# Seven block products for eight in the feed-forward stage of a two-layer hybrid backbone

## The chip, the core and the metric

The kernel runs as one program on one NeuronCore of a Trainium2 chip. The metric is the device time of one execution in microseconds (us). The engines are TensorE (PE in the profile; its weight loads are PEld), VectorE (DVE), ScalarE (ACT), GpSimd (POOL) and SyncE (SP), which here issues nearly all DMAs. Tiles live in SBUF with 128 partitions; TensorE writes to PSUM, which has eight banks of 128x512 float32.

## The reference

Two layers work on 1024 latent tokens and 256 context tokens of width 1024. Each layer modulates and norms its input, projects it, runs four mixers (convolution, gated linear attention, softmax attention, retention), projects back with w_out, and adds the feed-forward stage that the change is about:

```python
def sq_relu_mlp(h, w_up, w_down):
    return jnp.square(jax.nn.relu(h @ w_up)) @ w_down
...
        x = x + g1_l * o_l
        h2_l = rms_norm(x, norm2_g[l]) * (1.0 + sc2_l) + sh2_l
        x = x + g2_l * sq_relu_mlp(h2_l, w_up[l], w_down[l])
```

w_up is 1024x4096 and w_down 4096x1024. Layer 0 does the same for the context tokens; layer 1 does not need them. After layer 1 a final RMSNorm gives the output.

## The kernel before

Everything is held transposed: 128 features on the partitions, tokens along the row. Tokens come in three groups (TOK, line 29): the context (t = 0, 256 tokens) and two latent halves (t = 1 and 2, 512 each). Products are made at float32-like precision from rounded halves: split (line 180) lets ScalarE round a tile to its high part (line 181) and VectorE subtract that from the tile to give the low part (line 182); mm3 then takes three matmuls per 128x128 weight block: high with high, high with low, low with high (all of them show as line 188).

The feed-forward stage walks the hidden axis in 16 chunks of 256 rows (FC). For each chunk and each token group, up makes two 128-row blocks of hidden values in PSUM (8 x 3 matmuls each), lets ScalarE take relu and square (lines 1146 and 1147) and VectorE a second exact square and the low part (lines 1148 and 1149); down multiplies them with all eight 128-column blocks of w_down (2 x 3 matmuls each) and VectorE adds the gated result to x in SBUF (line 1162). The hidden values never leave the core. up of the next unit is issued ahead of down of the current one, so TensorE always has a unit to work on; five PSUM banks named bank rotate. Weights come in slabs of 128x1024 (load_slab), three staging buffers and five pairs of high and low parts.

The order on each engine is set by the program's text and by a scheduler that moves an instruction forward where its operands are ready; each engine then runs its list in order, waiting for semaphores. Buffers of a pool rotate: a new tile waits until the readers of the tile that had its place are done. SyncE issues DMAs in its list's order too.

In layer 0 the modulation matrix of layer 1 is computed in between (emit_mods, step(mg, 2)), and when a token group's last chunk is done, next_norm writes its normed input for layer 1 (lines 383, 386, 387). In layer 1 final_norm transposes and stores the output (line 1190). The output projection before the stage (line 1119) works in two halves of 512 columns.

## Time and profile before

| | |
|---|---|
| median of 3 runs | 3239.86 us (3232.47 to 3243.09) |
| the profiled execution | 3238.09 us, span 3236.3 us |
| mean granted TensorE clock | 0.957 of full speed |
| TensorE busy (matmuls) | 3034.6 us, 94% of the span |
| VectorE, ScalarE, GpSimd busy | 1670.9, 913.2 and 66.4 us |
| HBM traffic | 76 GB/s over the span |

The span runs from the first to the last instruction. A row of the profile names a line, an engine, an operation, and the tiles as output<-inputs. Busy shares of TensorE are of modelled matmul lengths that overlap in the pipe, so the rate is read from start to start. The granted clock is 1.00 at 2.4 GHz and 0.50 at 1.2 GHz.

### The profile page before, as it was taken

How to read it: one execution, taken by the hardware profiler on the slowest of the kernel's cores; microseconds unless marked ns; L12 is line 12 of the kernel's file. 1: busy time of each engine (PE TensorE's matmuls, PEld its weight loads, DVE VectorE, ACT ScalarE, POOL GpSimd, SP SyncE). 2: the span in 40 equal slices, each digit the busy share in tenths (PEclk: the TensorE clock that was granted, in tenths of full speed). 3: DMA queues.
4: the chain of work that ended last, by engine and by line, in shares of the span. 5: the costliest groups of instructions: out<-in, count | busy, mean ns of one | idle time of the engine just before them, and what ended most of it. 6: DMA issues, size and time to landing. Idle time of an engine off the chain costs nothing. (4 is left out here: it accounts for less than half of the span.)

```text
span 3236.3 us, 43494 instructions
## 1 busy us (share of the span) xinstructions
PE 3034.6 (94%) x18101; PEld 2452.4 (76%) x18101; DVE 1670.9 (52%) x2660; ACT 913.2 (28%) x1650; POOL 66.4 (2%) x114
## 2 busy tenths in 40 slices
...
GB/s 265 113 74 85 128 44 79 82 203 105 33 92 85 90 84 82 85 66 36 38 32 14 99 48 36 77 50 63 167 113 79 66 45 39 48 53 52 53 39 52
DMA packets 267230, 250.31 MB, mean 77 GB/s; under 512 B 28259, under 2 KB 227513, under 8 KB 267033
## 3 DMA queue, kind: packets, MB, share of 16 engines
...
q0 software_dynamic: 416, 0.92, 0.1%
q14 instruction: 56, 0.45, 0.0%
...
## 5 line engine op out<-in xcount | busy, mean ns | idle before, releaser
L188 PE MATMUL bank<-ahi,whi 128*128 128x512 f32 (+1 forms) x2096 | 787.5, 376 | 14.6 <-ACT ahi L181 11.2
L188 PE MATMUL bank<-ahi,wlo 128*128 128x512 f32 (+1 forms) x2096 | 777.8, 372 | 2.3 <-DVE wlo L182 2.3
L188 PE MATMUL bank<-alo,whi 128*128 128x512 f32 (+1 forms) x2096 | 779.5, 372 | 0.0
L1162 DVE SCALAR_TENSOR_TENSOR x<-bank,mods,x 128x512 f32<-128x512 f32 (+1 forms) x640 | 438.8, 695 | 248.0 <-PE bank L188 247.1
L188 PEld LDWEIGHTS bank<-ahi,whi 128*128 128x128 f32 x2096 | 397.5, 190 | 103.6 <-ACT ahi L181 14.3
L188 PE MATMUL bank<-hl,whi 128*128 128x512 f32 (+1 forms) x1280 | 471.8, 369 | 0.0
L188 PE MATMUL bank<-hh,whi 128*128 128x512 f32 (+1 forms) x1280 | 471.3, 368 | 0.0
L188 PE MATMUL bank<-hh,wlo 128*128 128x512 f32 (+1 forms) x1280 | 471.0, 368 | 0.0
L188 PEld LDWEIGHTS bank<-ahi,wlo 128*128 128x128 f32 x2096 | 396.9, 190 | 73.3 <-issue 5.9
L188 PEld LDWEIGHTS bank<-alo,whi 128*128 128x128 f32 x2096 | 397.7, 190 | 67.6 <-issue 5.4
L181 ACT CAST whi<-wst 128x1024 fp32r<-128x1024 f32 (+2 forms) x226 | 200.0, 895 | 668.6 <-PE bank L188 484.5
L182 DVE TENSOR_TENSOR wlo<-wst,whi 128x1024 fp32r<-128x1024 f32 (+2 forms) x226 | 231.6, 1036 | 278.9 <-ACT whi L181 276.1
L188 PEld LDWEIGHTS bank<-hl,whi 128*128 128x128 f32 x1280 | 241.4, 189 | 40.1 <-issue 0.2
L188 PEld LDWEIGHTS bank<-hh,wlo 128*128 128x128 f32 x1280 | 241.3, 189 | 40.2 <-issue 0.2
L188 PEld LDWEIGHTS bank<-hh,whi 128*128 128x128 f32 x1280 | 241.4, 189 | 40.0
L1146 ACT ACTIVATE tmp<-bank 128x512 f32<-128x512 f32 (+1 forms) x160 | 88.3, 552 | 647.9 <-PE bank L188 647.1
L1148 DVE TENSOR_TENSOR tmp<-tmp 128x512 f32<-128x512 f32 (+1 forms) x160 | 102.0, 638 | 305.1 <-ACT hh L1147 303.3
L188 PE MATMUL bank<-whi,ahi 128*128 128x256 f32 (+2 forms) x640 | 197.4, 309 | 12.2 <-ACT gqk L857 5.2
L188 PE MATMUL bank<-wlo,ahi 128*128 128x256 f32 (+2 forms) x640 | 192.1, 300 | 0.2 <-DVE wlo L182 0.2
L188 PE MATMUL bank<-whi,alo 128*128 128x256 f32 (+2 forms) x640 | 191.3, 299 | 0.0
L521 DVE SCALAR_TENSOR_TENSOR yacc<-u,wdw,yacc 128x1295 f32<-128x1295 f32 (+1 forms) x120 | 168.3, 1420 | 0.8
L691 DVE TENSOR_REDUCE amx<-S 128x1 f32<-128x1280 f32 (+1 forms) x72 | 98.7, 1371 | 131.2 <-PE S L188 126.3
...
## 6 DMA issues: line engine op xcount, KB each, us to landing
wm<-in_w_mod_dram SPq DMA_DIRECT2D x64, 512.0 KB, 3.7
wst<-in_w_up_dram SPq DMA_DIRECT2D x64, 512.0 KB, 4.0
wst<-in_w_down_dram SPq DMA_DIRECT2D x64, 512.0 KB, 4.4
...
wst<-in_w_out_dram SPq DMA_DIRECT2D x16, 512.0 KB, 5.3
...
```

The costliest lines, as they stand in the source:

```text
L181: nc.scalar.copy(hi, src)
L182: nc.vector.tensor_tensor(lo, src, hi.bitcast(F32), op=ALU.subtract)
L188: nc.tensor.matmul(ps, lhsT=lhsT, rhs=rhs, start=start, stop=stop)
L521: nc.vector.scalar_tensor_tensor(yv, uv, wv, yv, op0=ALU.mult, op1=ALU.add)
L691: nc.vector.reduce_max(mx[:, 0:1], S[:, 0:nk * 128], axis=AX.X)
L1146: nc.scalar.activation(rl[:, :n], b[:, :n], AF.Relu)
L1148: nc.vector.tensor_tensor(rl[:, :n], rl[:, :n], rl[:, :n], op=ALU.mult)
L1162: nc.vector.scalar_tensor_tensor(xt[t][:, d, :], b[:, :n], mod(l, 5, d, seg), xt[t][:, d, :], op0=ALU.mult, op1=ALU.add)
```

## The change

The stage is made in two phases, and each phase's product on the 1024 latent tokens is split into 2x2 blocks and computed by Strassen's scheme (in Winograd's form): weight blocks r11, r12, r21, r22, token blocks B11, B12, B21, B22, seven products named a11, a12, s2, s1, s3, s4 and a22 in their order, and sums of the blocks before and of the products after. All hidden values of the up phase go to a DRAM tensor hdram and are read back in the down phase. In up the token sums (T1 to T4) are made once per layer; in down the token side is the hidden values, so its differences (t2 and the in-place ones) are made in every chunk. A chunk is now 256 rows of each half of the hidden axis: 8 chunks per phase, 7 products per chunk, 24 matmuls of 512 columns per product. Context tokens (layer 0) are still multiplied in the plain way, with the weight parts of a11 and a12, and a22 and a21, and in layer 0 a step a21 exists for that.

Weight sums ta, tb and two differences are made by GpSimd on the staged weights (prep); the low parts of three of the seven hidden operands are made by GpSimd too. prep runs three products ahead (NW). Each weight and hidden pair has a slot of 8 KB per partition, shared with tiles of other stages; three weight slots (pw) and three hidden slots (a4, a5, a6) rotate, staged blocks have one buffer each. PSUM pairs of banks (w2) rotate three deep. Down keeps seven accumulators M of 128x2048, adds every product to its own by VectorE (line 1539), and combines them in the last chunk (dn_last). Further: each layer's output projection runs by 128 columns, x is kept in DRAM between, the first attention stage of layer 1 takes the token tiles 6 to 9 first, and the low parts of its weights are made by GpSimd.

```diff
...
+    def split(hi, lo, src, lo_eng=None):
         nc.scalar.copy(hi, src)
-        nc.vector.tensor_tensor(lo, src, hi.bitcast(F32), op=ALU.subtract)
+        (lo_eng or nc.vector).tensor_tensor(lo, src, hi.bitcast(F32), op=ALU.subtract)
...
+        def bank_pair():
+            return ps2.tile([128, 2, 512], F32, tag="w2", name="w2", bufs=3)
...
+        def out_rows(d, t):
...
+            acc_mm(b[:, :n], [(so[d][0][:, k, :], so[d][1][:, k, :], hi[:, k, :], lo[:, k, :]) for k in range(KD)], True, True)
+            nc.vector.scalar_tensor_tensor(xt[t][:, d, :], b[:, :n], mod(l, 2, d, 1 if t == 0 else 0), xt[t][:, d, :],
+                                           op0=ALU.mult, op1=ALU.add)
+            nc.sync.dma_start(out=xdram[:, d, o:o + n], in_=xt[t][:, d, :])
+            square(acc[t], xt[t][:, d, :], n, d == 0)
...
+        OPS = ["a11", "a12", "s2", "s1", "s3", "s4", "a22"] + (["a21"] if ctx else [])
+        steps = [(ph, c, op) for ph in ("up", "dn") for c in range(FP // 2) for op in OPS]
...
+        def load_raw(ph, c, tag):
+            R[ph, c, tag] = v = raw(tag)
+            i_, j_ = int(tag[1]) - 1, int(tag[2]) - 1
+            if ph == "up":
+                src = w_up[:, 4 * j_:4 * j_ + 4, 2048 * i_ + 256 * c:2048 * i_ + 256 * c + 256]
+                nc.sync.dma_start(out=v.rearrange("p (k n) -> p k n", k=4), in_=src)
+            else:
+                src = w_dn[:, FP * j_ + 2 * c:FP * j_ + 2 * c + 2, 512 * i_:512 * i_ + 512]
+                nc.sync.dma_start(out=v.rearrange("p (k n) -> p k n", k=2), in_=src)
...
+        h_tags = ("a4", "a5", "a6")
+        NW = 3
+
+        def prep(s_):
+            ph, c, op = steps[s_]
+            g = nc.gpsimd
+            r = {tg: R.get((ph, c, tg)) for tg in RAW}
+            if op == "a11":
+                r["ta"], r["tb"] = raw("ta"), raw("tb")
+                R[ph, c, "ta"], R[ph, c, "tb"] = r["ta"], r["tb"]
+            src = {"a11": "r11", "a12": "r12", "s2": "tb", "s1": "ta", "s3": "r11", "s4": "r12", "a22": "r22", "a21": "r21"}[op]
+            if op == "s3":
+                g.tensor_tensor(r["r11"], r["r11"], r["r21"], op=ALU.subtract)
+            if op == "s4":
...
+                p_ = ("pa", "b", "b")[(s_ - 2) % 3]
+                v = P[p_].tile([128, 2048], F32R, tag="pw", name="pw", bufs=1 if p_ == "pa" else 2)
+            split(v[:, 0:1024], v[:, 1024:2048], r[src])
+            wpair[s_] = pair_of(v, 4 if ph == "up" else 2)
+            if op == "a11":
+                g.tensor_tensor(r["ta"], r["r21"], r["r22"], op=ALU.add)
+                g.tensor_tensor(r["tb"], r["ta"], r["r11"], op=ALU.subtract)
+            for tg, when in (("r11", "s3"), ("r12", "s4"), ("r22", "a22"), ("r21", "a21" if ctx else "s3")):
+                if op == when:
+                    load_next(ph, c, tg)
+            if ph == "dn" and op != "a21":
+                h0_, h1_ = hraw[c]
+                b11, b12, b21, b22 = h0_[:, :, 0:512], h0_[:, :, 512:1024], h1_[:, :, 0:512], h1_[:, :, 512:1024]
+                if op == "a11":
+                    T["t2"] = P["b"].tile([128, 2, 512], F32, tag="t2", name="t2")
+                src = {"a11": b11, "a12": b21, "s2": T["t2"], "s1": b11, "s3": b12, "s4": b22, "a22": b21}[op]
+                m_ = c * 7 + OPS.index(op)
+                hv = pair_of(slot(h_tags[m_ % 3]), 2)
+                split(hv[0], hv[1], src, g if op in ("s2", "s3", "a22") else None)
+                hpair[s_] = hv
+                if op == "a11":
+                    g.tensor_tensor(b11, b12, b11, op=ALU.subtract)
+                    nc.vector.tensor_tensor(T["t2"], b22, b11, op=ALU.subtract)
+                if op == "a12":
+                    g.tensor_tensor(b21, b21, T["t2"], op=ALU.subtract)
+                    g.tensor_tensor(b12, b22, b12, op=ALU.subtract)
+                if op == "s3":
+                    load_hid(c + 2, 0)
+                if op == "a22":
...
+        def preps(s_):
+            n_ = done["prep"]
+            while n_ < len(steps) and n_ <= s_ + NW:
+                ph, c, op = steps[n_]
+                if n_ - NW >= 2 and held[n_ - NW] > s_:
+                    break
+                if ph == "dn" and op != "a21":
+                    m_ = c * 7 + OPS.index(op) - 3
+                    if m_ >= 0 and len(steps) // 2 + m_ // 7 * nstep + m_ % 7 > s_:
+                        break
+                prep(n_)
+                n_ += 1
+            done["prep"] = n_
...
+        for nm, tags in (("bigb", ["b3"]), ("bigc", ["b0", "b1"]), ("bigd", ["b2"])):
+            p_ = pools.get(nm, side="right", reuse_waits="tile")
+            SP.update({tg: p_ for tg in tags})
+        rstd(2)
+        T2, T1 = (half("a4"), half("a5")), (half("a6"), half("a7"))
+        B22, T4 = (half("b0"), half("b1")), (half("b2"), half("b3"))
+        s1, s2 = xt[1], xt[2]
+        for k in range(4):
+            lo_, hi_ = (slice(None), k, slice(None)), (slice(None), 4 + k, slice(None))
+            scaled(2, k)
+            scaled(2, 4 + k)
+            nc.gpsimd.tensor_tensor(s1[lo_], s2[lo_], s1[lo_], op=ALU.subtract)
+            t2_ = ntmp()
+            nc.vector.scalar_tensor_tensor(t2_, s2[hi_], sh2(4 + k), s1[lo_], op0=ALU.add, op1=ALU.subtract)
+            split(T2[0][:, k, :], T2[1][:, k, :], t2_)
+            nc.vector.scalar_tensor_tensor(s1[hi_], s1[hi_], sh2(4 + k), t2_, op0=ALU.add, op1=ALU.subtract)
+        for k in range(4):
...
+        def up_step(s_, c, op):
...
+            wh, wl = wpair[s_]
+            for f in range(2):
+                fs = slice(f * 128, (f + 1) * 128)
+                psb[f] = half_bank()
+                acc_mm(psb[f], [(wh[:, k, fs], wl[:, k, fs], rh[:, k, :], rl[:, k, :]) for k in range(4)], True, True)
+            for f in range(2):
...
+                u2, u4 = keep.get(("u2", f)), keep.get(("u4", f))
+                plus = lambda o_, i_: nc.vector.tensor_tensor(o_, i_, b, op=ALU.add)
+                if op == "a11":
+                    keep["u2", f] = nacc()
+                    nc.scalar.copy(keep["u2", f], b)
+                elif op == "s2":
+                    plus(u2, u2)
+                elif op == "s1":
+                    keep["u4", f] = u4 = P["u"].tile([128, 512], F32, tag="u4", name="u4", bufs=3)
+                    plus(u4, u2)
+                else:
+                    if op == "a12":
+                        v = ntmp()
+                        plus(v, u2)
+                    elif op == "s4":
+                        v = u4
+                        plus(v, v)
+                    else:
+                        v = P["u"].tile([128, 512], F32, tag="uo", name="uo", bufs=3)
+                        plus(v, u4 if op == "s3" else u2)
+                        if op == "s3":
+                            plus(u2, u2)
+                    relu2(v)
+                    hid_out(v, hi_f if op in ("s3", "a22") else lo_f, 1 if op in ("s3", "s4") else 0)
...
+        ACC = {"a11": "a7", "a12": "b4", "s2": "b2", "s1": "a8", "s3": "b0", "s4": "b1", "a22": "b5"}
...
+        def dn_last(op, jj, b):
+            v = M[op]
+            if op in ("s4", "a22"):
+                for j in (2 * jj, 2 * jj + 1):
+                    d, t = (j, 2) if op == "s4" else (4 + j, 1)
+                    gated(v[:, j, :], b[:, j % 2, :], d, v[:, j, :])
...
+                add(nc.vector, "s1", "s2")
+                add(nc.gpsimd, "a22", "s2")
+            elif op == "s1":
+                add(nc.vector, "s4", "s1")
+            elif op == "s3":
+                add(nc.vector, "a22", "s3")
+                add(nc.vector, "s3", "s1")
+                blocks("s4", 0, 2, False)
...
+        def dn_step(s_, c, op):
+            if op == "a21":
+                dn_ctx(c, 1, (wpair[s_], wpair[s_ - 1]))
+                ctx_split(c + 1)
+                return
+            wh, wl = wpair[s_]
+            rh, rl = hpair[s_]
+            for jj in range(2):
+                b = bank_pair()
+                for j in range(2):
+                    ds = slice((2 * jj + j) * 128, (2 * jj + j + 1) * 128)
+                    acc_mm(b[:, j, :], [(wh[:, f, ds], wl[:, f, ds], rh[:, f, :], rl[:, f, :]) for f in range(2)], True, True)
+                js = slice(2 * jj, 2 * jj + 2)
+                if c == 0:
+                    if jj == 0:
+                        M[op] = slot(ACC[op]).bitcast(F32).rearrange("p (k n) -> p k n", k=4)
+                    nc.scalar.copy(M[op][:, js, :], b)
+                elif c < FP // 2 - 1:
+                    nc.vector.tensor_tensor(M[op][:, js, :], M[op][:, js, :], b, op=ALU.add)
+                else:
+                    dn_last(op, jj, b)
+            if ctx and op == "a12":
+                dn_ctx(c, 0, (wpair[s_ - 1], wpair[s_]))
...
+        def ending(t):
...
+                final_norm(t)
+            elif t == 0:
+                h[0] = (ctx_rows("a8"), ctx_rows("a9"))
+                norm_mod(1, 0, x0, 0, h[0], acc[0])
+            else:
+                j0 = 0 if t == 2 else 4
+                h[t] = tuple(Rows(half(f"a{j}"), half(f"a{j + 1}")) for j in (j0, j0 + 2))
+                norm_mod(1, 0, xout[t], t, h[t], acc[t])
...
```

What stands on VectorE in layer 1's stage: before, a row of a unit's eight additions to x, and squarings and low parts between them (wlo are weights, hl hidden values).

```order
L1148 TENSOR_TENSOR tmp<-tmp 128x512
L1162 SCALAR_TENSOR_TENSOR x_20124<-bank,mods_93,x_20124 128x512
L1149 TENSOR_TENSOR hl<-tmp,hh 128x512
L1162 SCALAR_TENSOR_TENSOR x_20124<-bank,mods_93,x_20124 128x512 x7
L182 TENSOR_TENSOR wlo<-wst,whi 128x1024 x3
```

Now, in one down chunk of layer 1 from the preparation of a11 on: pw and a_ are low parts of weights and hidden values, b_22576 is the accumulator of s4 and b_22613 that of a22, w_ are pairs of banks, t_23081 is t2.

```order
L182 TENSOR_TENSOR pw<-r_22962,pw 128x1024
L182 TENSOR_TENSOR a_23082<-a_22708,a_23082 128x1024
L1539 TENSOR_TENSOR b_22576<-b_22576,w_23087 128x1024
L1266 TENSOR_TENSOR t_23081<-a_22783,a_22708 128x1024
L1539 TENSOR_TENSOR b_22576<-b_22576,w_23101 128x1024
L182 TENSOR_TENSOR pw<-r_23003,pw 128x1024
L182 TENSOR_TENSOR a_23118<-a_22783,a_23118 128x1024
L1539 TENSOR_TENSOR b_22613<-b_22613,w_23123 128x1024
L1539 TENSOR_TENSOR b_22613<-b_22613,w_23137 128x1024
L182 TENSOR_TENSOR pw<-tb,pw 128x1024
```

The additions to x became additions of whole products, and t2 (line 1266) stands between the two of product s4.

GpSimd had nothing in the stage before. Now it has, in the same chunk of layer 1 (ta and tb are the weight sums, L1238 and L1240 differences of weights, L1265, L1269 and L1268 those of hidden blocks, L182 low parts of t2 and two hidden blocks):

```order
L1249 TENSOR_TENSOR ta<-r_22964,r_23039 128x1024
L1250 TENSOR_TENSOR tb<-ta,r_22962 128x1024
L1238 TENSOR_TENSOR r_22962<-r_22962,r_22964 128x1024
L1265 TENSOR_TENSOR a_22708<-a_22708 128x2x512
L1269 TENSOR_TENSOR a_22708<-a_22783,a_22708 128x2x512
L1240 TENSOR_TENSOR r_23003<-r_23003,tb 128x1024
L1268 TENSOR_TENSOR a_22783<-a_22783,t_23081 128x2x512
L182 TENSOR_TENSOR a_23154<-t_23081,a_23154 128x1024
L182 TENSOR_TENSOR a_23227<-a_22708,a_23227 128x1024
L182 TENSOR_TENSOR a_23302<-a_22783,a_23302 128x1024
```

In a chunk of layer 0 the same work stands in another order:

```order
L1265 TENSOR_TENSOR a_11351<-a_11351 128x2x512
L1269 TENSOR_TENSOR a_11351<-a_11438,a_11351 128x2x512
L1249 TENSOR_TENSOR ta<-r_11902,r_11858 128x1024
L1250 TENSOR_TENSOR tb<-ta,r_11770 128x1024
L1238 TENSOR_TENSOR r_11770<-r_11770,r_11902 128x1024
L1268 TENSOR_TENSOR a_11438<-a_11438,t_11945 128x2x512
L182 TENSOR_TENSOR a_12061<-t_11945,a_12061 128x1024
L1240 TENSOR_TENSOR r_11816<-r_11816,tb 128x1024
```

In layer 1 the weight sums come first, and the difference that t2 reads (L1265) is fourth; in layer 0 it is first.

## Rows read from the trace of the kernel before

**Rows 1.** The page: span, busy us (share of the span) and instructions of each engine.

```profile
span 3236.3 us, 43494 instructions
...
PE 3034.6 (94%) x18101; PEld 2452.4 (76%) x18101; DVE 1670.9 (52%) x2660; ACT 913.2 (28%) x1650; POOL 66.4 (2%) x114
```

**Rows 2.** Windows by stage, columns in the first row (x = instructions).

```profile
core 0: us, PE busy (x) PEld busy (x) DVE busy (x) ACT busy (x) POOL busy (x), PEclk, DMA share, GB/s
905.00:1802.00 897.00, 897.00 (x4899) 756.41 (x4898) 442.44 (x696) 178.31 (x281) 0.00 (x0) 1.00 0.21 63
1802.00:1845.00 43.00, 25.06 (x104) 22.15 (x103) 31.04 (x52) 20.95 (x41) 1.02 (x8) 0.56 0.46 128
...
2514.00:3203.00 689.00, 688.13 (x3032) 568.48 (x3032) 349.94 (x460) 149.21 (x207) 0.00 (x0) 1.00 0.15 46
```

**Rows 3.** Chain that ended last: start us, length us, engine, tile and line, count.

```profile
2521.65 681.70 PE bank L188 x3005
```

**Rows 4.** Timeline of TensorE at 890 us: start us, length us, engine, line, operation.

```profile
890.20 0.28 PE L188 MATMUL bank<-ahi,whi 128*128 128x256 f32 x1
...
891.63 0.28 PE L188 MATMUL bank<-ahi,whi 128*128 128x256 f32 x1
```

**Rows 5.** Groups by shape, VectorE and ScalarE: busy us, mean ns of one, idle before.

```profile
L1162 DVE SCALAR_TENSOR_TENSOR x<-bank,mods,x 128x512 f32<-128x512 f32 x512 | 380.3, 749 | 187.5 <-PE bank L188 186.7
...
L182 DVE TENSOR_TENSOR wlo<-wst,whi 128x1024 fp32r<-128x1024 f32 x144 | 173.9, 1222 | 241.5 <-ACT whi L181 240.8 <-PE bank L188 0.2
L181 ACT CAST whi<-wst 128x1024 fp32r<-128x1024 f32 x144 | 149.4, 1051 | 594.2 <-PE bank L188 456.3 <-DMA wst<-in_w_up_dram 113.7 <-DMA wst<-in_w_out_dram 18.0
...
L1148 DVE TENSOR_TENSOR tmp<-tmp 128x512 f32<-128x512 f32 x128 | 88.4, 692 | 245.1 <-ACT hh L1147 243.5
...
L709 DVE COPY apT<-pt 128x512 f32<-128x512 f32 x66 | 45.4, 689 | 71.1 <-PE pt L185 71.0
...
L387 DVE SCALAR_TENSOR_TENSOR alo<-tmp,mods,ahi 128x512 fp32r<-128x512 f32 x64 | 45.8, 747 | 5.0 <-ACT ahi L386 2.4
...
L383 DVE SCALAR_TENSOR_TENSOR tmp<-x,msc,acc 128x512 f32<-128x512 f32 x64 | 45.4, 745 | 8.9 <-ACT acc L175 8.9
...
L725 DVE TENSOR_TENSOR adg<-ident,als 128x256 f32<-128x256 f32 x36 | 14.8, 450 | 10.0 <-PE pt L188 9.9
...
L1045 DVE TENSOR_TENSOR rab<-sc,c_retm 128x512 f32<-128x512 f32 x18 | 12.3, 690 | 50.7 <-PE sc L188 50.7
...
L387 DVE SCALAR_TENSOR_TENSOR alo<-tmp,mods,ahi 128x256 fp32r<-128x256 f32 x24 | 10.7, 482 | 1.6 <-ACT ahi L386 1.6
...
L383 DVE SCALAR_TENSOR_TENSOR tmp<-x,msc,acc 128x256 f32<-128x256 f32 x24 | 10.6, 479 | 3.6 <-ACT acc L175 3.6
```

**Rows 6.** The same by shape, GpSimd.

```profile
L536 POOL TENSOR_TENSOR tmp<-tmp 128x512 f32<-128x512 f32 x4 | 5.5, 1380 | 19.0 <-ACT tmp L535 19.0
...
L536 POOL TENSOR_TENSOR tmp<-tmp 128x256 f32<-128x256 f32 x1 | 0.7, 731 | 16.7 <-ACT tmp L535 16.7
```

**Rows 7.** Timeline, GpSimd and VectorE at 111 us; idle before it in brackets.

```profile
111.53 0.83 POOL L616 TENSOR_TENSOR asq<-gain,ass 128x384 f32<-128x384 f32 x1 [5.91 <-DVE ass L615]
...
112.99 0.56 DVE L628 TENSOR_TENSOR asq<-arw,cosa 128x384 f32<-128x384 f32 x1
113.03 1.40 POOL L627 TENSOR_TENSOR at<-arw,sina 128x384 f32<-128x384 f32 x1 [0.67 <-DVE arw L621]
```

**Rows 8.** Timeline, GpSimd and VectorE at 2062 us.

```profile
2062.09 1.84 DVE L725 TENSOR_TENSOR adg<-ident,als 128x256 f32<-128x256 f32 x2
...
2062.32 1.33 POOL L529 TENSOR_TENSOR tmp<-yacc 128x512 f32<-128x512 f32 x1 [154.92 <-DVE yacc L521]
...
2068.66 1.27 POOL L536 TENSOR_TENSOR tmp<-tmp 128x512 f32<-128x512 f32 x1 [5.00 <-ACT tmp L535]
...
2068.88 0.69 DVE L709 COPY apT<-pt 128x512 f32<-128x512 f32 x1 [1.88 <-PE pt L185]
```

**Rows 9.** Instructions on tile asq: duration ns min/median/max, first and last start.

```profile
L628 DVE TENSOR_TENSOR asq<-arw,cosa x16: 557/558/1182, 103.1 to 1904.7; 128x384 f32<-128x384 f32 x16
```

**Rows 10.** The page's DMA issues: KB each, median us from issue to landing.

```profile
wst<-in_w_down_dram SPq DMA_DIRECT2D x64, 512.0 KB, 4.4
```

**Rows 11.** Windows of 2 us, columns as in rows 2.

```profile
2354.00:2356.00 2.00, 1.25 (x24) 0.84 (x24) 0.00 (x0) 0.58 (x1) 0.00 (x0) 1.00 0.90 328
2356.00:2358.00 2.00, 0.00 (x0) 0.00 (x0) 1.22 (x1) 1.52 (x3) 0.00 (x0) 0.72 1.01 345
2358.00:2360.00 2.00, 0.00 (x0) 0.00 (x0) 1.23 (x1) 1.95 (x2) 0.00 (x0) 0.50 0.95 351
2360.00:2362.00 2.00, 1.96 (x3) 0.93 (x4) 0.00 (x0) 0.00 (x0) 0.00 (x0) 0.50 0.92 320
2362.00:2364.00 2.00, 2.00 (x5) 0.50 (x5) 0.00 (x0) 0.09 (x1) 0.00 (x0) 0.58 0.66 251
2364.00:2366.00 2.00, 1.80 (x16) 1.12 (x14) 0.70 (x2) 2.00 (x3) 0.00 (x0) 1.00 0.00 0
```

451 lines of the change are left out of this document (326 added, 125 removed).

## The prediction

> **What bounds the kernel now.** I read the page first: TensorE is busy 94% of the span, VectorE 52%, GpSimd 2% [rows 1]. The windows by stage come next. The reader is to see that both feed-forward stretches, 905 to 1802 us in layer 0 and 2514 to 3203 us in layer 1, have TensorE busy for practically every microsecond at the full granted clock, with VectorE about half busy and GpSimd at zero [rows 2]. The chain of waits says the same of layer 1: 3005 matmuls in one unbroken piece of 681.70 us [rows 3], so one 128x512 matmul costs 681.70 / 3005 = 0.2269 us from start to start (the 0.39 us in its own row is its length in the pipe). A 128x256 one costs (891.63 - 890.20) / 12 = 0.119 us [rows 4]. The stage is bound by the number of matmuls, and everything else has room beside them. The change takes matmuls away and spends that room.
>
> **What is saved.** Per layer the latent tokens take 8 x 32 x 3 matmuls of 512 columns for each token half in up and as many in down: 4 x 768 = 3072. Seven block products for eight leave 2688. So each layer loses 384 and each of the four phases (up and down, two layers) 192, which is 43.6 us; all four 768 x 0.2269 = **174.3 us**. The context rows in layer 0 (1536 matmuls of 256 columns, 182.8 us) and the modulation matmuls stay. A chunk (256 rows of the hidden axis pair, seven products of 24 matmuls, 5.45 us each) takes TensorE 38.1 us, in layer 0 with context and modulation about 50.6.
>
> **What is added, against that room.** Prices: a VectorE pass over 128x1024 from SBUF is 1.22 us, over 128x512 0.69, the same 0.69 when one input is in PSUM (rab<-sc), a scalar_tensor_tensor 0.75; ScalarE's rounding copy of 128x1024 is 1.05 [rows 5]. GpSimd takes 1.27 for an addition of 128x512 [rows 8] and 0.73 for one of 128x256 [rows 6]; 128x1024 is in no row, so I estimate 1.27 + 2 x 0.54 = 2.35.
>
> Up, per chunk: 14 additions from PSUM (9.7), 8 squarings (6.0) and 7 low parts (8.5) are 24.2 us of VectorE, and 4 GpSimd passes are 9.4. Even laid end to end these are 33.6, under 38.1. Nothing on VectorE waits for GpSimd but the low parts of the weight sums, which are made more than two products ahead. The writes of the hidden rows and the larger traffic (2 MB out and 2 MB in per chunk, against 46 GB/s and a DMA share of 0.15 now [rows 2]) stay well inside 38 us. Up costs nothing beyond its matmuls; if its cover went, the price would be the few microseconds of one late weight pair per chunk.
>
> Down, layer 1, per chunk: 14 additions from PSUM of 128x1024, 7 low parts of weights, 4 of hidden blocks and the difference T2: 26 x 1.22 = 31.7 us of VectorE. GpSimd: 4 weight sums, 3 hidden differences, 3 low parts: 10 x 2.35 = 23.5. Here the two collide. A GpSimd addition of 128x384 takes 0.83 alone and 1.40 when a VectorE multiplication of 0.56 began 0.04 us before it: 0.83 + 0.56 [rows 7]. The other way round the same multiplication, 0.56 normally, once took 1.18 [rows 9], and two 0.45 us ones took 1.84 beside a GpSimd addition [rows 5, 8]. So passes with two SBUF inputs run one after the other with GpSimd's. A VectorE copy from PSUM beside a GpSimd addition changed neither (0.69 and 1.27) [rows 5, 8]; I take additions with one input in PSUM to be free too. The Trainium skill says both: "SBUF — State Buffer", section "Who interferes with whom", calls it an exclusive lock that a VectorE instruction takes with two SBUF inputs against a GpSimd one that reads SBUF, and not with one. By the part that no row shows (one input in PSUM) the additions are free and the sum stands as below; without it the fourth rival's time would follow.
>
> Twelve of VectorE's 26 passes (14.7 us) exclude GpSimd's 23.5: 38.2 us of one port for 38.1 of TensorE. That alone is a tie; order decides. In the listed order T2 stands between the two PSUM additions of product s4, and GpSimd comes to the difference that T2 reads after two weight sums and a difference of weights. Those wait for block r22, which is fetched only when the old r22 has been split. From the end of product s1 (0): r22 split at 2.5, landed 4.4 us later [rows 10] at 6.9; then low part, sum, low part, sum, and two differences take turns until 18.5, GpSimd's next difference is queued and takes the port until 20.9, T2 is done at 22.1 and the second addition of s4 at 23.3. TensorE finished a22 at 16.3 and has no free pair of banks: the next matmul starts at 23.3. VectorE then works off what queued up (two low parts, two additions of a22, two of a11, ...) and TensorE gets bank pairs at its pace: the next s1 ends at 47.8, not 38.1. Without the collision the same chain gives 41.6. So 9.7 us are lost per chunk, bounds 3.5 and 11.7. The upper bound adds the clock: an idle stretch of 4 us (2356 to 2360) left it at half for about 4 us more [rows 11], worth 2 us. I take 9.7, since rows show the collision. Chunk 0 has the differences ahead of the weight sums, and the last is counted below, so it is paid six times: **-58.2** (21 to 70).
>
> Down, layer 0: GpSimd's order has the hidden differences ahead of the weight sums, so T2 comes in time; VectorE needs 28 x 1.22 + 8 x 0.48 = 38.0 of 50.6. Two low parts (tb and the context block) stand ahead of those of a12, which makes a12 about 3 us late: 7 x 3 = **-21** (0 to 68, the upper end being layer 1's loss in each chunk).
>
> Last chunk, layer 1: 7 low parts (8.5), 10 additions (12.2), five sums of 128x2048 (2.3 each, 11.5) and 24 scalar_tensor_tensor (18) are 50.2 of VectorE, with some 10 of turns with GpSimd 60; then a square, GpSimd's addition, the reciprocal root, eight output rows at 0.75 and the store, some 20: 80 us. Before, matmuls worth 38.1 and what follows (2514 + 697 = 3211 to the end at 3236.3, 25.3) are 63.4: **-16.6** (-5 to -30). Layer 0's last chunk is as heavy, but already before TensorE stood or ran at half clock from 1802 to 1845 [rows 2] behind the norms: **-8** (0 to 15).
>
> Start of up: T2's operand needs, after the last output row, 4.5 us of norm and 4 x (4 x 0.75 + 0.69) = 14.8 of VectorE; a11 and a12 hide 10.9 of the 19.3, in layer 0 the context 5.7 more: **-8.4** and **-2.7** (0 to 15 together). The shared slots, the order of the attention tiles and the split low parts of w_in on GpSimd I cost at nothing, hidden beside the norms in 1802 to 1845.
>
> **Sum.** 174.3 - 58.2 - 21 - 16.6 - 8 - 8.4 - 2.7 = 59.4, from the profiled 3238.1 to 3178.7; the median of the runs is 1.8 higher than the profiled one, so 3180.
>
> **Rivals.** (1) The cover holds: GpSimd and VectorE overlap, as they have slack on average (31.7 and 23.5 of 38.1). Only the starts and ends are paid: 174.3 - 35.7 = 138.6, 3101. For it: the port sum is a tie, and a faster GpSimd pass would break it. Against: the listed order. (2) Slower: both down phases run at the pace of the port and the clock drops at each stall. Layer 0 loses 9.7 in each of seven chunks (47 more) and 13 stalls cost 2 us each of half clock (26): 3253. It decides when the down chunks of both layers are on average more than 10 us over their matmuls. For it: layer 0 has the same 23.5 us on GpSimd and more on VectorE. Against: 12 us more of TensorE work per chunk to hide it, and the better order. (3) The junctions eat it: all three norms of layer 0 (8 x 1.49 us of VectorE for each half, 8 x 0.96 for the context, 31.5 [rows 5]) now follow the last product, where the latent half 768 to 1279 alone did. If attention waits for two of them, 25 us: 3205. Against: the tiles of the half whose norm comes first are now first. (4) Every VectorE pass, additions from PSUM included, excludes GpSimd: 55.2 us per chunk in layer 1 and 61.5 in layer 0, 17.1 x 8 and 10.9 x 8 lost in place of 58 and 21: 3325. Against: the copy beside the addition at 2068 [rows 8].
>
> **Chances.** Likeliest 0.50 (its own range 3145 to 3215), (1) 0.27, (2) 0.14, (3) 0.05, (4) 0.04. Range 3090 to 3240: below it lies the lower edge of (1), 0.06, above it (4) and most of (2), 0.13. About 0.3%, 10 us, is what a measurement of this kernel tells from no change. Of (2) 0.03 falls within that, 0.02 of it ends faster; so faster 0.84, same 0.03, slower 0.13.
>
> **What would show it.** Right: up phases with TensorE busy throughout, 38 us per chunk in layer 1; in layer 1's down phase gaps of about 7 us on TensorE, ended by a VectorE addition of s4, VectorE's own idle time before T2 ended by GpSimd, GpSimd passes from 2.35 to 3.6 us, chunks of some 48 us; layer 0's down chunks near 54. Wrong: chunks of 38 us in layer 1's down phase (rival 1), gaps in layer 0's (rival 2), or a pass from PSUM that is stretched beside GpSimd (rival 4).

## The result, and the profile after

The changed kernel takes 3324.06 us (median of 4 runs, 3320.89 to 3329.9), the kernel before in the same session 3236.35. The ratio is 1.0271, with a 95% interval of 1.0246 to 1.0296: slower by 88 us where I had forecast 56 us faster. The profiled executions differ by 82.6 us (3318.9 against 3236.3).

The page's engine line answers to [rows 1]: TensorE has 768 matmuls less to do and still is busy for a smaller share of a longer span; VectorE and GpSimd have taken over work.

```profile
PE 2963.5 (89%) x17333; PEld 2315.3 (70%) x17333; DVE 2060.0 (62%) x2557; ACT 1042.7 (31%) x1678; POOL 800.1 (24%) x405
```

The windows of the changed kernel (span, then busy time and count by engine, granted clock, DMA share, GB/s) answer to [rows 2]: the steady part of layer 0's up, layer 0's down, layer 1's up, layer 1's down; then layer 1's last chunk with the tail, and layer 0's with the junction.

```profile
1034.00:1301.00 267.00, 258.52 (x1323) 215.55 (x1322) 144.89 (x150) 57.55 (x70) 55.60 (x21) 0.98 0.26 89
1393.00:1744.00 351.00, 341.42 (x1930) 260.94 (x1923) 251.38 (x238) 99.30 (x99) 162.06 (x61) 1.00 0.43 137
2641.00:2876.00 235.00, 235.00 (x1008) 189.33 (x1008) 160.62 (x174) 50.06 (x54) 59.62 (x24) 1.00 0.32 107
2952.00:3173.00 221.00, 205.38 (x833) 159.06 (x831) 192.63 (x127) 69.67 (x70) 147.29 (x51) 0.96 0.27 95
...
3218.00:3319.00 101.00, 62.94 (x248) 48.39 (x248) 82.03 (x68) 20.49 (x30) 50.94 (x23) 0.75 0.23 78
1750.00:1910.00 160.00, 101.14 (x516) 82.73 (x514) 121.55 (x142) 53.40 (x96) 73.69 (x51) 0.80 0.26 73
```

The reader is to see three things. Layer 1's up is unbroken (235.00 of 235.00 busy), yet holds 1008 matmuls, one in 0.2331 us, where [rows 3] has one in 0.2269. Layer 0's up, which has more TensorE work to hide behind, is not unbroken. And the two end windows have TensorE busy for under two thirds, at a granted clock of 0.75 and 0.80.

Adding up, over each stage, the distances between matmul starts beyond 0.2267 us (0.1197 for 256 columns) gives the places of the loss, in us of TensorE standing or at half clock (a few missing records can make these a little too large):

| stage | forecast | measured |
|---|---|---|
| start of up, layer 0 (880 to 985) / layer 1 (2560 to 2646) | 2.7 / 8.4 | 28.1 / 25.1 |
| rest of up, layer 0 (985 to 1305) / layer 1 | 0 / 0 | 20.0 / 0 |
| down, layer 0 (1305 to 1745) | 21 | 31.0 |
| down, layer 1 (2890 to 3220) | 58.2 | 37 |
| last chunk and junction, layer 0 (1745 to 1877) | 8 above before's | 70.4 (before, 1797 to 1820: 17.2) |
| last chunk and tail, layer 1 | 16.6 | 35 (from the last chunk's first matmul at 3220.60: 98.3 to the end, for the 80 forecast; the forecast's own 63.4 for the kernel before is taken off) |
| matmuls of 512 columns further apart, all stages | 0 | 37, less some 10 for those of 256 |

Two groups carry most of the miss: the starts and ends of the phases (forecast 36, measured about 140 over before's), and a pace of the matmuls that was in no term. With before's own losses taken off (17.2 at the junction, 6 or 7 in layer 0's down), the rows add up to some 250 us, of the 257 that the 174.3 saved and the 82.6 lost make.

The waits of TensorE in layer 0's last chunk and junction (us in total, times, the longest), 1745 to 1878 of the changed kernel:

```profile
PE bank L188 <- POOL wm L1447: 19.1, 1, 19.1
PE w L188 <- DVE b L1459: 10.7, 6, 5.6
PE bank L188 <- POOL acc L1447: 9.7, 2, 5.6
```

Line 1447 adds up the squares for the norms on GpSimd, acc for the latent halves and wm for the context. So 29 of the 70 us are waits for these sums; in the longest of them VectorE also makes the eight rows of one latent half's norm (1850.7 to 1869). Before, TensorE's longest wait there, from 1797 to 1821, was for the sum of one norm:

```profile
PE c L188 <- DVE acc L370: 14.1, 1, 14.1
```

And layer 1's last chunk on TensorE, with a passage of GpSimd and VectorE in it (in brackets the wait):

```profile
3220.60 15.82 PE L188 MATMUL w<-a,pw 128*128 128x512 f32 x60 [2.88 <-ACT a L181]
3239.67 14.07 PE L188 MATMUL w<-a,pw 128*128 128x512 f32 x48 [3.26 <-DVE b L1493]
3262.17 13.14 PE L188 MATMUL w<-a,pw 128*128 128x512 f32 x48 [8.43 <-DVE a L1493]
```

```profile
3231.82 5.58 POOL L1496 TENSOR_TENSOR b<-b,a 128x2048 f32<-128x2048 f32 x1
3232.87 5.62 DVE L182 TENSOR_TENSOR a<-a,a 128x1024 fp32r<-128x1024 f32 x1
```

Two of the sums of whole products (line 1496, 128x2048) are GpSimd's. Behind this one a low part of 1.22 us took 5.62.

### The profile page after: what moved, and what is told of

It reads as the page before. It is cut to its first block, busy times and chain, and to the rows that moved or that the text cites. A ratio compares the mean times of both kernels' runs of the same rounds, so it can differ in the third digit from the quotient of the medians.

```text
span 3318.9 us, 43252 instructions
## 1 busy us (share of the span) xinstructions
PE 2963.5 (89%) x17333; PEld 2315.3 (70%) x17333; DVE 2060.0 (62%) x2557; ACT 1042.7 (31%) x1678; POOL 800.1 (24%) x405
## 4 chain that ended last, share of the span: by engine, by line
PE 52%; DVE 14%; issue 5%; POOL 4%; DMA 4%; ACT 3%; SPq 0%; POOLq 0%; ACTq 0%; DVEq 0%
PE w L188 34%; PE bank L188 9%; DVE pw L182 2%; DVE a L182 2%; PE ob L188 2%; PE sc L188 2%; PE S L188 2%; PE pt L185 1%; DVE b L1539 1%; PE s L188 1%; POOL a L1265 1%; PE oo L188 1%; DVE b L1474 1%; POOL tb L1250 1%; POOL a L182 1%
## 5 line engine op out<-in xcount | busy, mean ns | idle before, releaser
L188 PE MATMUL w<-a,pw 128*128 128x512 f32 (+1 forms) x5592 | 1209.2, 376 | 107.3 <-DVE b L1459 17.0
L188 PEld LDWEIGHTS w<-a,pw 128*128 128x128 f32 x5592 | 964.4, 195 | 349.0 <-DVE b L1459 29.3
L181 ACT CAST pw<-r 128x1024 fp32r<-128x1024 f32 x171 | 179.5, 1050 | 580.3 <-PE w L188 511.2
L182 DVE TENSOR_TENSOR pw<-r,pw 128x1024 fp32r<-128x1024 f32 x171 | 251.3, 1470 | 56.1 <-ACT pw L181 56.1
L188 PE MATMUL w<-b,pw 128*128 128x512 f32 x1128 | 267.6, 396 | 1.3 <-DVE u L1397 1.3
L188 PEld LDWEIGHTS w<-b,pw 128*128 128x128 f32 x1128 | 210.7, 188 | 55.6 <-DVE u L1397 5.6
L188 PE MATMUL w<-a,whi 128*128 128x512 f32 (+1 forms) x640 | 189.0, 382 | 16.0 <-ACT a L181 13.2
L1539 DVE TENSOR_TENSOR b<-b,w 128x1024 f32<-128x1024 f32 x120 | 143.7, 1213 | 32.2 <-PE w L188 31.5
L182 POOL TENSOR_TENSOR a<-a,a 128x1024 fp32r<-128x1024 f32 x32 | 82.2, 2568 | 253.1 <-ACT a L181 244.3
L188 PE MATMUL bank<-whi,a 128*128 128x256 f32 (+2 forms) x640 | 133.1, 299 | 10.9 <-ACT aov L606 7.7
L188 PE MATMUL bank<-a,whi 128*128 128x512 f32 (+1 forms) x416 | 134.7, 401 | 5.4 <-ACT aov L606 5.4
L182 DVE TENSOR_TENSOR a<-a,a 128x1024 fp32r<-128x1024 f32 x64 | 126.2, 1971 | 1.2 <-ACT a L181 1.2
L1240 POOL TENSOR_TENSOR r<-r,tb 128x1024 f32<-128x1024 f32 x32 | 86.3, 2698 | 124.0 <-DVE pw L182 112.3
```

The costliest lines, as they stand in the source:

```text
L181: nc.scalar.copy(hi, src)
L182: (lo_eng or nc.vector).tensor_tensor(lo, src, hi.bitcast(F32), op=ALU.subtract)
L188: nc.tensor.matmul(ps, lhsT=lhsT, rhs=rhs, start=start, stop=stop)
L1240: g.tensor_tensor(r["r12"], r["r12"], r["tb"], op=ALU.subtract)
L1539: nc.vector.tensor_tensor(M[op][:, js, :], M[op][:, js, :], b, op=ALU.add)
```

## The experiments

Each ratio in brackets is to the kernel before, with its 95% interval.

### The matmuls' pace

A matmul's two operands are its weights and the moving operand, the tile that streams past them. The tiles of the left side of SBUF (the weights among them) lie 64 bytes off in the changed kernel: a tile of 1024 bytes per partition among the constants (mev) is gone and two small ones (dsh) have come. So the moving operand's address less the weights', modulo 512 bytes, is 448 for all feed-forward products on pw tiles, and was 0. (The 128-column blocks of a weight tile lie 512 bytes apart, so this remainder is the same for all of them.)

**e1_left64**, the left side moved by 64:

```
+    cpool.tile([128, 16], F32, name="shift")
```

> An unused tile of 64 bytes per partition behind the constants moves every tile on the left side of SBUF by 64 bytes, so that the weight tiles lie at a multiple of 128 bytes again, as in the kernel before (in the changed kernel they lie 64 past one). Nothing else changes. Theory 1, the address sets the matmul's pace: 512-column matmuls come 0.2267 us apart in place of 0.2333; summed over the unbroken ones of the trace that is 37 us more than before in the changed kernel, less some 8 that the 256-column ones gain by the shift, so about 3290 to 3300, and an up chunk of layer 1 takes 38.1 us in place of 39.2. Rival, the pace comes from the traffic or from high and low parts in one tile: 3324 and 39.2.

3321.78 us (1.0278, 1.0257 to 1.0298): theory 1 in this form fell. An up chunk of layer 1 takes 39.04 us for 39.2, the matmuls come 0.2324 us apart. The edit made the difference 384, not 0.

**e2_before_left64**, the same line in the kernel before.

> The kernel before with the same unused 64 bytes: its left side now lies 64 past a multiple of 128. Theory 1: its 512-column matmuls go from 0.2267 to 0.2333 us apart, 6100 of them in the feed-forward alone, about 40 us, less about 10 for the 256-column ones: 3260 to 3275. Rival: 3236.

3257.95 us (1.0082, 1.0067 to 1.0097), 26 us slower. Here the up products, whose weights moved and whose moving operand did not (448), come 0.2333 us apart and the down products, where both moved (0), 0.2272. So neither address alone sets the pace.

**e3_right64**, the right end moved as well:

```
-    pools.get("pad", side="right").tile([128, 120], F32, name="pad")
+    pools.get("pad", side="right").tile([128, 136], F32, name="pad")
```

> The changed kernel with 64 bytes more of padding at the right end of SBUF, so that weights (left) and moving operands (right) both lie 64 past a multiple of 128. If the weights' address alone sets the pace: 3324. If it is that the two differ: 3290 to 3300. If both count: above 3324, up chunk of layer 1 over 39.2.

3326.76 us (1.0293, 1.0278 to 1.0308); difference 384 and 0.2325 us as in e1_left64, though both tiles lie elsewhere.

**e5_pad104**, the right end moved the other way, by a padding of `[128, 104]`: difference 0.

> The changed kernel with 64 bytes less of padding at the right end of SBUF: moving operand and weights of the feed-forward's matmuls then lie at the same address modulo 512, as in the kernel before. In the changed kernel they differ by 448 (0.2333 us from one matmul to the next), in e1_left64 and e3_right64 by 384 (0.2325). Theory 1b, the difference modulo 512 sets the pace: 0.2267, an up chunk of layer 1 in 38.1 us; 5376 x 0.0066 = 35 us less where TensorE runs unbroken, 256-column matmuls back at 0.119 for 0.115 (some 7 us): 3295 to 3302. Rival, two tiles side by side or the traffic: 3322 to 3327.

3305.24 us (1.0219, 1.0193 to 1.0246). The stretches of one chunk on TensorE in layer 1's up (start, length, count), first of the changed kernel, then of this one:

```profile
2640.83 16.96 PE L188 MATMUL w<-a,pw 128*128 128x512 f32 x72
2657.63 16.96 PE L188 MATMUL w<-b,pw 128*128 128x512 f32 x72
```

```profile
2686.35 16.48 PE L188 MATMUL w<-b,pw 128*128 128x512 f32 x72
2702.67 17.62 PE L188 MATMUL w<-a,pw 128*128 128x512 f32 x77
```

From start to start 72 matmuls take 16.80 us and 16.32 us: 0.2333 and 0.2267. Theory 1b holds: the chunk takes 38.1 us, as forecast, and the whole gains 19 us (35 less 7 were expected where TensorE runs unbroken; in a stalled stage the waits take part of it back: a chunk of layer 1's down goes from 44.5 to 43.9 us, 0.6 for the 1.1 that its 168 matmuls gain).

### Layer 0's up

**e6_relu_act**, on e5_pad104:

```
-            nc.vector.scalar_tensor_tensor(v, v, 0.0, v, op0=ALU.max, op1=ALU.mult)
+            nc.scalar.activation(v, v, AF.Relu)
+            nc.scalar.activation(v, v, AF.Square)
```

> As e5_pad104, and the squared relu in up is made by two ScalarE passes in place of one VectorE pass with SBUF inputs. Theory 3: in layer 0 the context's second product waits 2 us in each chunk for a bank, because the squarings ahead of its eviction stand 2.8 us behind GpSimd's weight sums for 0.69, and half the clock after it costs 2 more; with the squarings gone the chunks of layer 0's up fall from 54 to 49.5 to 50.5: 20 to 28 us less than e5_pad104. Rival, the bank comes late because of the number of evictions: 54, no gain.

3286.82 us (1.0161, 1.0139 to 1.0183), 18 us less; layer 0's chunks fall from 54 to 50.4. The changed kernel's rows of VectorE, GpSimd and TensorE (start, length, engine, and in brackets the wait) show why:

```profile
1070.22 2.89 DVE L1367 SCALAR_TENSOR_TENSOR u<-u 128x512 f32<-128x512 f32 x1
1073.03 0.68 DVE L1397 TENSOR_TENSOR uo<-acc,w 128x512 f32<-128x512 f32 x1
1073.74 2.16 DVE L1367 SCALAR_TENSOR_TENSOR uo<-uo 128x512 f32<-128x512 f32 x1
1075.83 0.68 DVE L1397 TENSOR_TENSOR uo<-acc,w 128x512 f32<-128x512 f32 x1
```

```profile
1069.13 3.42 POOL L1249 TENSOR_TENSOR ta<-r,r 128x1024 f32<-128x1024 f32 x1 [34.22 <-DVE u L1397]
1072.64 2.71 POOL L1250 TENSOR_TENSOR tb<-ta,r 128x1024 f32<-128x1024 f32 x1
...
1076.56 24.10 PE L188 MATMUL w<-a,pw 128*128 128x256 f32 x144 [2.05 <-DVE uo L1397]
```

A squaring reads SBUF alone and takes 0.69 us by itself; beside GpSimd's sum it took 2.89 and 2.16. The addition behind it, which frees a bank, is late, and TensorE waits 2.05 us for the context's product (8.1 us in four such waits from 1034 to 1301). Shortly after it the granted clock falls to half: the first eleven of the 256-column matmuls come about 0.118 us apart, the next 16 about 0.213. The window of those 4 us shows it (columns as above, the granted clock is the 0.68):

```profile
1076.50:1080.50 4.00, 3.94 (x24) 3.94 (x25) 2.16 (x2) 0.00 (x0) 1.64 (x1) 0.68 0.34 131
```

Layer 1 has no context product there and did not wait. The edit takes the whole pass off VectorE, not the stretch alone; that the stretch is what counts is read from the rows.

### Layer 1's down

**e4_no_hidden_diff**, on e1_left64, GpSimd's three differences of hidden blocks left out:

```
-                    g.tensor_tensor(b11, b12, b11, op=ALU.subtract)
-                    nc.vector.tensor_tensor(T["t2"], b22, b11, op=ALU.subtract)
+                    nc.vector.tensor_tensor(T["t2"], b22, b12, op=ALU.subtract)
...
-                    g.tensor_tensor(b21, b21, T["t2"], op=ALU.subtract)
-                    g.tensor_tensor(b12, b22, b12, op=ALU.subtract)
```

> As e1_left64, and GpSimd's three hidden differences per down chunk are left out (products s3, a22, s4 get raw blocks, T2 on VectorE reads two raw blocks; the output is not the reference's). GpSimd keeps four weight sums and three low parts. Theory 2, layer 1's down is set by the chain b11's low part, GpSimd's difference, T2: its chunks fall from about 43.5 to 38.1 to 39, layer 0's by at most 2, together some 30 to 45 us under e1_left64. Rival, VectorE and GpSimd share the port and its sum decides: 7 passes of 2.4 to 3.4 us stay, chunks stay above 41.

3291.78 us (1.0181, 1.0162 to 1.0200), 30 less; chunks 39.5 us, with matmuls worth 39.04. It fits the chain to T2, but also fewer passes on GpSimd.

**e7_diff_first**, on e5_pad104, the order alone:

```
+            def sums(behind=None):
+                i_ = g.tensor_tensor(r["ta"], r["r21"], r["r22"], op=ALU.add).ins
+                if behind is not None:
+                    after_(i_, behind)
+                g.tensor_tensor(r["tb"], r["ta"], r["r11"], op=ALU.subtract)
...
+                    sums(first)
```

> As e5_pad104, and in down GpSimd makes the first hidden difference (which T2 reads) ahead of the two weight sums. The same passes, another order. Theory 2 (the chain to T2 sets layer 1's down): chunks from some 43.5 to 38.1 to 40 us, 20 to 35 us less than e5_pad104. Rival, the port's sum of VectorE and GpSimd passes: chunks stay above 42, less than 8 us gained.

3311.46 us (1.0237, 1.0212 to 1.0263), chunks 43.9 as before the edit: my chain theory fell. T2's wait for GpSimd went from 3.5 to 1.4 us, and T2 itself from 1.22 to 3.40. In the changed kernel TensorE has one long gap in each chunk, as here, where 156 matmuls run on unbroken after it:

```profile
3176.14 38.25 PE L188 MATMUL w<-a,pw 128*128 128x512 f32 x156 [2.89 <-DVE b L1539]
```

The groups of VectorE in layer 1's down (busy us, mean ns, idle before) of the changed kernel, 2995 to 3173:

```profile
L1539 DVE TENSOR_TENSOR b<-b,w 128x1024 f32<-128x1024 f32 x40 | 47.5, 1211 | 8.1 <-PE w L188 8.1
L182 DVE TENSOR_TENSOR pw<-r,pw 128x1024 fp32r<-128x1024 f32 x20 | 43.1, 2153 | 0.0
L182 DVE TENSOR_TENSOR a<-a,a 128x1024 fp32r<-128x1024 f32 x16 | 34.9, 2183 | 0.0
...
L1266 DVE TENSOR_TENSOR t<-a,a 128x1024 f32<-128x1024 f32 x4 | 4.9, 1225 | 14.1 <-POOL a L1265 14.1
```

The same of e7_diff_first, 2980 to 3156:

```profile
L182 DVE TENSOR_TENSOR a<-a,a 128x1024 fp32r<-128x1024 f32 x16 | 36.9, 2305 | 0.0
L182 DVE TENSOR_TENSOR pw<-r,pw 128x1024 fp32r<-128x1024 f32 x20 | 32.8, 1641 | 0.0
...
L1270 DVE TENSOR_TENSOR t<-a,a 128x1024 f32<-128x1024 f32 x4 | 13.6, 3405 | 5.5 <-POOL a L1269 5.5
```

**e9_no_weight_sums**, on e7_diff_first, GpSimd's four weight sums left out in down:

```
-                    sums(first)
...
-            if op == "s3":
+            if op == "s3" and ph == "up":
                 g.tensor_tensor(r["r11"], r["r11"], r["r21"], op=ALU.subtract)
```

> As e7_diff_first, where the difference for T2 came first and layer 1's chunks still took 43.9 us, and GpSimd's four weight sums per down chunk are left out (products get raw blocks, so the output is not the reference's). The chain b11's low part, GpSimd's difference, T2 stays as it is. Theory 5, the turns: TensorE waits because VectorE's passes with two SBUF inputs (T2, two low parts) take 2.2 to 3.4 us for 1.22 behind a run of GpSimd passes, and the additions from PSUM are queued behind them: chunks 38.1 to 40, 25 to 35 us less. Theory 2, the chain itself: 43 to 44, no gain.

3245.5 us (1.0027, 1.0010 to 1.0043), 66 us less than e7_diff_first; layer 1's chunks take 38.1 us with no gap. The same groups from 2956 to 3147:

```profile
L182 DVE TENSOR_TENSOR pw<-r,pw 128x1024 fp32r<-128x1024 f32 x35 | 48.9, 1396 | 0.0
L182 DVE TENSOR_TENSOR a<-a,a 128x1024 fp32r<-128x1024 f32 x20 | 24.3, 1215 | 0.0
...
L1271 DVE TENSOR_TENSOR t<-a,a 128x1024 f32<-128x1024 f32 x6 | 7.4, 1225 | 8.3 <-POOL a L1270 8.3
```

T2 still waits 8.3 / 6 = 1.4 us per chunk; what is gone is the stretch: the hidden low parts go from 2.3 us to 1.2, T2 from 3.4 to 1.2, and those of weights from 1.64 to 1.40. In the changed kernel the stretch of the low parts was 5 x 0.93 + 4 x 0.96 = 8.5 us of VectorE per chunk, and the additions that free the banks stand behind it. The profiled executions differ by 61 us: 42 lie between the first and the last T2 of layer 1, 14 in layer 0 and 7 behind the last T2, less 2 before the stage.

**e10_t2_gpsimd**, the edits of e5_pad104, e6_relu_act and e8_start (which follows below) together and T2 on GpSimd too:

```
-                    nc.vector.tensor_tensor(T["t2"], b22, b11, op=ALU.subtract)
+                    first = g.tensor_tensor(T["t2"], b22, b11, op=ALU.subtract).ins
```

> The edits of e5_pad104, e6_relu_act and e8_start together, and in down the first difference and T2, both on GpSimd, ahead of the weight sums. From e6_relu_act 3287 and e8_start's 6 us: 3281 where nothing else changes. Theory 5, the place: T2 no longer stands in VectorE's queue ahead of the additions that free the banks; layer 1's chunks 39 to 41.5, 3260 to 3268. Rival, the sum of the passes on the port (GpSimd now has 11 per chunk, 27 us): chunks 43 to 45, 3278 to 3290.

3290.93 us (1.0174, 1.0152 to 1.0195): the rival was nearer, and even its 43 to 45 us were too few. T2 recurs every 48 us (2988.47, 3036.53, 3084.55), and TensorE now waits for a low part of GpSimd (9.0 us in three chunks) and for an addition (7.3). Taking T2 out of VectorE's queue did not help; but GpSimd also has one pass more, so the place alone was not tested.

Set side by side, the four edits go with the sum of what takes turns. An estimate, with GpSimd's passes at 2.40 us and VectorE's passes with two SBUF inputs at 1.22, their times without a stretch: 29.0 us per chunk in e9_no_weight_sums, which has no gap; 31.4 in e4_no_hidden_diff, chunks 39.5 with matmuls worth 39.04; 38.6 in the changed kernel and in e7_diff_first, chunks 44.5 and 43.9; 39.8 in e10_t2_gpsimd, chunks 48. From 38.6 on the chunk is longer by some 5 us or more than this sum and than its matmuls. How the excess comes about, turn by turn, no run took apart.

### The start of up, and down without block products

**e8_start**, on e5_pad104:

```
-            nc.gpsimd.tensor_tensor(s1[lo_], s2[lo_], s1[lo_], op=ALU.subtract)
+            nc.vector.tensor_tensor(s1[lo_], s2[lo_], s1[lo_], op=ALU.subtract)
...
                     prep(3)
-                    done["prep"] = 4
+                    prep(4)
+                    done["prep"] = 5
```

> As e5_pad104; at the start of up the four differences of x go from GpSimd to VectorE, and in layer 1 the low part of s3's weights is made ahead of the operands T3, B22 and T4. Theory 4, the start is bound by VectorE's chain of passes and its turns with GpSimd: first chunk from 64 to 50 to 57 us in layer 1 and from 78 to 68 to 74 in layer 0, 10 to 20 us in all. Rival, ScalarE's copy of a11's second half, which waits for the buffer of the norm's sum, holds TensorE: no gain.

3299.34 us (1.0199, 1.0173 to 1.0224), 6 us less, about as much as the runs tell apart. a11's second copy follows the first after 18.3 us for 21.1. Rows of the changed kernel at layer 1's start:

```profile
2575.08 0.40 PE L188 MATMUL w<-a,wlo 128*128 128x512 f32 x1
2575.32 2.44 PE L188 MATMUL w<-a,a 128*128 128x512 f32 x10
...
2577.78 1.12 PE L188 MATMUL bank<-acc,ones 128*128 128x512 f32 x2
2578.34 5.15 PE L188 MATMUL w<-a,a 128*128 128x512 f32 x20
...
2581.21 1.68 POOL L1351 TENSOR_TENSOR x<-x,x 128x512 f32<-128x512 f32 x1 [39.34 <-issue]
...
2584.03 1.77 DVE L1312 SCALAR_TENSOR_TENSOR x<-x,msc,acc 128x512 f32<-128x512 f32 x1
...
2598.09 1.70 DVE L182 TENSOR_TENSOR a<-tmp,a 128x512 fp32r<-128x512 f32 x1
2598.11 0.29 PEld L188 LDWEIGHTS w<-a,pw 128*128 128x128 f32 x1 [4.80 <-ACT a L181]
```

TensorE ends the output projection at 2575 and has only 30 of the 48 matmuls of a11 and a12 left (5.15 and 2.44 us): the other 18 already stood between the last output rows (at 2560.03). The norm's sum is ready at 2577.8, and T2's four blocks take until 2599.8, with passes of 0.74 us stretched to 1.77 beside GpSimd's.

In layer 0 the longest wait at the start, from 880 to 985, is the one that the rival named, for ScalarE's copy of a11's second half; in e8_start it is 6.6 us:

```profile
PE w L188 <- ACT acc L1400: 9.4, 1, 9.4
```

**e11_plain_down**: the edits of e5_pad104, e6_relu_act and e8_start, and the seven products in up alone. The core of its down:

```
+                    acc_mm(b[:, j, :], [(w_[0][:, f, ds], w_[1][:, f, ds], h_[0][:, f, :], h_[1][:, f, :])
+                                        for w_, h_ in ((wdn[4 * c + 2 * i_ + q], hdn[4 * c + 2 * (t - 1) + q]) for q in range(2))
+                                        for f in range(2)], True, True)
```

> The edits of e5_pad104, e6_relu_act and e8_start together; up by seven products as in the changed kernel, down through DRAM by eight plain block products, accumulated over both hidden halves in PSUM (192 matmuls per chunk for 168, 8 additions of 128x1024 for 14, no GpSimd pass, no sums after the last product). If what the seven products save in down (43.6 us per layer) goes into VectorE and GpSimd: layer 1's chunks 43.5 without a gap (43.9 now), its tail 20 to 30 us shorter; layer 0's chunks 61 (57.7 now, 26 us more), its junction 25 to 35 us shorter; 3215 to 3265 against 3281. If the tails and junctions are long for another reason (norms, loads of x): 3290 to 3310.

3235.98 us (1.0004, 0.9988 to 1.0019), level with the kernel before. Against 3281 for the same kernel with the seven products in down (estimated from e6_relu_act and e8_start, not run), the seven products in down save 87 us of matmuls in both layers and cost some 132. A chunk of layer 1's down takes 43.5 us without them and without a gap, for 43.9 with them. And the 87 us of matmuls that the products save in up are spent as well; some 39 of them are lost at its two starts (19.8 and 19.5 us, added up as in the table). Its last 65 us answer to the tail of the changed kernel:

```profile
3170.00:3235.00 65.00, 50.13 (x236) 40.63 (x234) 24.29 (x34) 9.81 (x18) 18.23 (x14) 0.89 0.19 73
```

The gap is in layer 1: from the first copy of its up to the end 696 us, in e10_t2_gpsimd 746. Layer 0 is even, 1635.6 and 1640.0 us from first copy to first copy: its down chunks are 4 to 5 us longer, the junction shorter. There the longest wait of the changed kernel, 19.1 us for the context's sum and the same in e10_t2_gpsimd, is down to

```profile
PE bank L188 <- POOL wm L1424: 3.7, 1, 3.7
```

**e12_short_start**, on e11_plain_down: rows scaled and subtracted before the norm is known.

```
-            scaled(2, k)
-            scaled(2, 4 + k)
-            nc.vector.tensor_tensor(s1[lo_], s2[lo_], s1[lo_], op=ALU.subtract)
+            nc.vector.tensor_tensor(s2[hi_], s2[hi_], acc[2], op=ALU.mult)
             t2_ = ntmp()
-            nc.vector.scalar_tensor_tensor(t2_, s2[hi_], sh2(4 + k), s1[lo_], op0=ALU.add, op1=ALU.subtract)
+            nc.vector.scalar_tensor_tensor(t2_, s2[hi_], sh2(4 + k), s1[lo_], op0=ALU.add, op1=ALU.add)
```

> As e11_plain_down (3236), and less of the start of up depends on the second half's norm: the rows of x are scaled by the norm's gain and subtracted (e = upper minus lower rows) while the output projection still runs, so that after the norm T2 takes 3 VectorE passes per block (0.69 + 0.75 + 0.69, 8.5 us in all) in place of 5 or 6 with turns (18 us measured from the norm to the last of T2); T1, T3, B22 and T4 follow from the same product. Theory 4, the start waits for this chain: TensorE's gaps and half clock at the start, 28 us in layer 0 and 25 in layer 1 in the changed kernel, fall by 6 to 12 us each: 3212 to 3226. Rival, the wait moves on to T1, T3 and T4, which VectorE makes next: under 4 us gained in all, 3230 to 3238.

3231.09 us (0.9989, 0.9978 to 0.9999), some 5 us less, though the two intervals overlap, and between the two expectations. The copies of a11 are 15.0 and 14.7 us apart for 18.3, but TensorE's loss at the start goes only from 19.8 to 18.9 us in layer 0 and from 19.5 to 16.1 in layer 1: it now waits 7.7 us for a weight pair in layer 0, and in layer 1 3.5 us for an addition that VectorE makes behind T3, B22 and T4. The wait moved on, as the rival said.

**e13_short_start_r1**: the token halves in the order (1, 2) for the upper rows of the last chunk.

```
-                for t in (2, 1) if end else (1, 2):
+                for t in (2, 1) if end and i_ else (1, 2):
```

> As e12_short_start; in down's last chunk the upper output rows take the token halves in the order of the other chunks (first half first), so that the last low part of the hidden rows is not waited for. Expected 2 to 4 us less in each layer than e12_short_start if that low part is late, nothing if the bank or the norm is.

3230.53 us (0.9985, 0.9974 to 0.9995): no difference from e12_short_start. It is the fastest version here, ahead of the kernel before by 0.15%, which is less than what separates single runs.

## Why the prediction was wrong

The step that failed most is the one that priced the starts and the ends of the phases: 35.7 us in the forecast, about 140 measured. Next come two things that were put at nothing, up's rest (20) and the distance of the matmuls (27). Only layer 1's down, the largest term, was paid less than forecast.

**The saving of 174.3 us** is there in matmuls, at 0.2267 us each. The step that all terms shared, that a matmul keeps its distance, failed: it depended on an address that the change shifted by the way, which cost some 19 us in the end (e5_pad104).

**"Up costs nothing beyond its matmuls"** failed in layer 0. I laid VectorE's 24.2 us and GpSimd's 9.4 us end to end against 38.1 and concluded from the sum; I named the late weight pair as the only price. What came late was a bank, behind squarings stretched from 0.69 to 2.9 us, in the product that the context adds: 18 us (e6_relu_act).

**The start of up, -8.4 and -2.7**, came to 25 and 28, a miss of 42 us. The chain after the last output row took 23.5 us for 19.3 (2576.3 to 2599.8): the norm was about as forecast (4.0), T2's blocks took 19.5 for 14.8, stretched by GpSimd's passes. Two more parts of the term failed: a11 and a12 do not hide 10.9 us of it, because 18 of their 48 matmuls stand between the output rows, and behind T2 the next operands (T1, T3, B22, T4) are made on the same engine, so that further waits follow. e8_start, with fewer of GpSimd's passes there, shortens layer 1's first chunk from 63.5 to 57.4 us, and e12_short_start shows the last part: a shorter chain moved the wait. In layer 0 the longest wait was for a copy that the term left out. Some 35 us at the two starts no run took away.

**Down, layer 1, -58.2**: the forecast collision is there, GpSimd's passes of 2.4 to 3.4 us, the wait for T2 of 3.5 and the gaps on TensorE. Chunks take 44.5 us, not 47.8, and at the old pace 43.9: 5.8 lost each, not 9.7. I had chained T2 after everything that GpSimd does since r22's landing; e7_diff_first shows that the loss stays when T2's difference comes first, and e9_no_weight_sums that it goes when GpSimd has fewer passes to take turns with. The Trainium skill, "SBUF — State Buffer", section "Who interferes with whom", says that issue order decides who blocks; the trace agrees: here another order gave the wait to another pass and the chunk the same 43.9 us.

**Down, layer 0, -21** was near (31.0 with the 6 or 7 that before lost too), but not for the reason given. TensorE's waits from 1458 to 1745 add up to only 5 us, about 1 in each chunk, and they end with VectorE's additions of the context and of products, not with a12's low parts. The chunks take 57.7 us, not near 54: the 50.6 of matmuls in them was too low for the modulation's (seven runs of 0.64 us in a chunk), which the kernel before pays too.

**The last chunks, -16.6 and -8**, are the largest miss: 35 and over 50. In layer 1 I took 60 us of VectorE and 20 after it; GpSimd's sums of 128x2048 stretch passes by up to 4 us (1.22 to 5.62), and TensorE stood 8.43 us in the middle of the chunk. (The 25.3 us of before's tail was too long as well: its last matmul of the stage starts at 3218.8, not 3211.) For layer 0 I set VectorE's work against a time in which TensorE "already stood" at the junction [rows 2]; it stood for 17.2 us, and the new last chunk, its sums and the norms take 70, of which 29 are TensorE's waits for the norms' sums on GpSimd. The low parts of w_in, which I put at nothing, stand among these sums in GpSimd's list. Down without the products has shorter ends in both layers (e11_plain_down), which shows the source; what each part of it costs was not tested.

**The rivals.** The fourth, that additions from PSUM too exclude GpSimd (3325), hit the time and is wrong: these additions take 1211 ns in the worst stretch, and 1218 in e11_plain_down, where GpSimd is idle. The second (3253) named the port and the clock, but layer 0's down, on which it rested, was not the place. The first, that the cover holds, would need chunks of 38.1 us in layer 1's down, and they take 44.5. The third, that the norms behind the last product hold up layer 0's junction, named a place that counted, but at 25 us, where it is 53 over before's. What no rival had was that the starts, ends and junctions together take about 140 of the 174 us that the products save.
